# Row sums in fp32: own tiles for the pairs of the last row, and a one-element copy that takes over a wait

## Chip, cores, metric

One NeuronCore of one Trainium2 chip. The metric is device time in microseconds (us) of one execution. The runs were taken on several chips; a ratio always compares runs of the same rounds on one chip.

## The reference

```python
batch, seq, dim = 32, 512, 1024          # x: float32, normally distributed

def reference(x):
    return np.sum(x, axis=-1).astype(np.float32)
```

There are 16,384 rows of 1024 numbers, 67.1 MB to read and 64 KB to write.

## The kernel before

Each of the 128 partitions takes 128 rows, in seven tiles of 16 rows and a last tile of 16 rows that is loaded in shrinking pieces. VectorE and ScalarE sum the rows of each piece as it lands. The very last row of every partition (row 15 of the last tile) comes in two pieces that meet at column `CUT`. VectorE sums each by pairs: it adds the left half of a piece to the right half and accumulates the sums. The first sum leaves its result in `part`; the second starts from `part` and writes the final value.

```python
CUT = 576

    def pairs_dve(xt, a, b, first, acc):
        h = (a + b) // 2
        nc.vector.tensor_tensor_reduce(
            out=xt[:, a:h], in0=xt[:, a:h], in1=xt[:, h:b], scale=1.0, scalar=first,
            op0=ADD, op1=ADD, accum_out=acc,
        )
    # ... cut: the seven full tiles, and pieces of 8, 4, 2 and 1 rows of the last tile ...
    last = 15 * D
    for i, k in ((0, CUT), (CUT, D)):
        nc.sync.dma_start(
            out=xt[:, last + i : last + k],
            in_=x_b[:, c * D + last + i : c * D + last + k],
        )
    # ... cut: sums of the other rows of the last tile ...
    pairs_dve(xt, last, last + CUT, 0.0, part)
    pairs_dve(xt, last + CUT, last + D, part, res[:, c + 15 : c + 16])
    nc.sync.dma_start(out=out_b, in_=res)
```

A semaphore is a counter that a load or an engine raises when its work is done, and on which an instruction can wait. The compiled program gives each of the two sums two semaphore waits: one for its load and one for VectorE's own earlier work. In the first sum the second wait comes from writing the pairs back into `xt`; in the second it covers both that and `part`.

## Time and profile before

| | before |
|---|---|
| time, median of the three runs first given | 162.29 us (162.26 to 162.44) |
| span of the profiled run | 160.5 us |
| VectorE busy | 76% |
| HBM read | 67.11 MB |
| last load lands | 157.633 us |
| final store issued | 158.292 us |

These lines of the page of the kernel before show the busy share of each engine, the busy tenths of the DMA engines in 40 slices of the span, and the bytes moved.

```profile
DVE 122.7 (76%) x14; ACT 16.0 (10%) x29; POOL 0.2 (0%) x4
...
DMA  9979996996996996996996996996997998999991
...
HBM read 67.11 MB, written 0.07 MB: 418 GB/s over the span
```

The DMA engines are busy, or close to it, until the 39th slice ends (156.5 us). VectorE is idle for a quarter of the span. The kernel is bound by its loads.

The next lines are the end of the chain of work that ended last: start in us, duration in us, what. DVE is VectorE and ACT is ScalarE; a "q" marks an instruction of an engine's sequencer, which issues its instructions, and SPq issues the loads and the final store.

```profile
118.20 38.90 DMA xt<-in_x_dram
157.10 0.03 issue
157.13 0.02 DVEq L57
157.15 0.09 issue
157.24 0.46 DVE xt L57
157.70 0.02 DVE part L57
157.72 0.05 issue
157.77 0.45 DVE xt L57
158.22 0.01 DVEq L114
```

The first piece of the last row lands at 157.10. Then 0.14 us pass before the first sum starts at 157.24, with a short instruction of VectorE's sequencer ("DVEq") among them. That instruction is one of the two waits; both sums have one:

```profile
L57 DVEq EVENT_SEMAPHORE  x2: 21/21/21, 157.1 to 157.7; - x2
```

In the trace it holds the wait for the load, and the sum itself holds the wait for VectorE's own work.

The timeline of the same stretch has start, duration, engine, line, operation and sizes, and in brackets the idle time before.

```profile
157.24 0.46 DVE L57 CUSTOM_DVE_ANT_0 xt<-xt 128x288 f32<-128x288 f32 x1 [0.93 <-DMA xt<-in_x_dram]
...
157.62 0.08 DVE L57 DVE_READ_ACCUMULATOR2_ANT part<- 128x1 f32 x1
157.77 0.45 DVE L57 CUSTOM_DVE_ANT_0 xt<-xt,part 128x224 f32<-128x224 f32 x1
158.14 0.08 DVE L57 DVE_READ_ACCUMULATOR2_ANT res<- 128x1 f32 x1
158.29 0.35 SPq L108 DMA_DIRECT2D out_dram<-res  x1
```

Each paired sum is two instructions: the sum, and a read of its accumulator.

I use three measures throughout. They are taken to the nanosecond from the trace's instruction records and semaphore updates. L1 and L2 are the times at which the two pieces of the last row have landed (the last of the sixteen updates of that load's semaphore). The **tail** is the time from L2 to the issue of the final store: 158.292 - 157.633 = 0.659 us before.

### The profile page before, as it was taken

To read this page: it belongs to the slowest core of one execution; us is meant where nothing else is said; L and a number is where in the kernel's file an instruction comes from. 1 tells how busy PE (TensorE), PEld (TensorE's weight loads), DVE (VectorE), ACT (ScalarE), POOL (GpSimd) and SP (SyncE) were. 2 spreads that over 40 slices of the span, in tenths; PEclk is the share of its full clock that TensorE was granted. 3 is DMA by queue.
4 is the path that set the end of the run, shared out by engine and by line. 5 is a ranking of instruction groups with operands and counts; after the bars stand their busy time and mean duration, and the time that the engine had idled before them with its cause. 6 is when DMAs were issued, how large, how long until landed. Compare 5 with 4: busy or idle time off the path is not lost.

```text
span 160.5 us, 118 instructions
## 1 busy us (share of the span) xinstructions
DVE 122.7 (76%) x14; ACT 16.0 (10%) x29; POOL 0.2 (0%) x4
## 2 busy tenths in 40 slices
DVE  0000059997799959999499994999949998699992
ACT  0000000000000000000000000000000000692892
POOL 0000000000000000000000000000000000000000
DMA  9979996996996996996996996996997998999991
GB/s 376 490 306 429 490 523 261 523 523 261 523 523 261 523 523 261 523 523 261 523 523 261 523 506 278 523 506 278 523 474 310 523 425 359 392 425 425 419 401 46
DMA packets 2304, 67.18 MB, mean 418 GB/s; under 512 B 512, under 2 KB 640, under 8 KB 1024
## 3 DMA queue, kind: packets, MB, share of 16 engines
q1 hardware_dynamic: 2160, 67.12, 97.3%
q10 hardware_dynamic: 144, 0.06, 0.1%
HBM read 67.11 MB, written 0.07 MB: 418 GB/s over the span
## 4 chain that ended last, share of the span: by engine, by line
DMA 74%; DVE 22%; SPq 1%; issue 0%; DVEq 0%
DMA xt<-in_x_dram 74%; DVE res L41 21%; SPq L93 1%; DVE xt L57 1%; DVEq L57 0%; DVE part L57 0%; DVEq L114 0%
## 5 line engine op out<-in xcount | busy, mean ns | idle before, releaser
L41 DVE TENSOR_REDUCE res<-xt 128x16 f32<-128x16384 f32 (+4 forms) x10 | 121.8, 12203 | 34.5 <-DMA xt<-in_x_dram 34.5
L49 ACT ACT_TABLE_LOAD x1 | 1.3, 1283 | 137.9 <-DMA xt<-in_x_dram 137.9
L49 ACT ACTIVATE xt<-xt 128x1024 f32<-128x1024 f32 x14 | 14.6, 1042 | 3.7 <-DVE res L41 3.7
L49 ACT ACTIVATION_READ_ACCUMULATOR xt<-xt 128x1 f32 x14 | 2.6, 186 | 0.0
L57 DVE CUSTOM_DVE_ANT_0 xt<-xt 128x288 f32<-128x288 f32 x1 | 0.5, 459 | 0.9 <-DMA xt<-in_x_dram 0.9
L57 DVE CUSTOM_DVE_ANT_0 xt<-xt,part 128x224 f32<-128x224 f32 x1 | 0.5, 452 | 0.1
L151 POOL MEMSET const-uint8-127<- 128x1 uint8 x1 | 0.1, 102 | 0.0
L151 POOL MEMSET const-bfloat16-1.0<- 128x1 bf16 x1 | 0.1, 101 | 0.0
L151 POOL MEMSET const-float32-0.0<- 128x1 f32 x1 | 0.1, 98 | 0.2 <-issue 0.2
L151 POOL MEMSET const-float32-1.0<- 128x1 f32 x1 | 0.1, 98 | 0.0
L57 DVE DVE_READ_ACCUMULATOR2_ANT res<- 128x1 f32 x1 | 0.1, 84 | 0.0
L57 DVE DVE_READ_ACCUMULATOR2_ANT part<- 128x1 f32 x1 | 0.1, 83 | 0.0
## 6 DMA issues: line engine op xcount, KB each, us to landing
xt<-in_x_dram SPq DMA_DIRECT2D x1, 7680.0 KB, 21.3
xt<-in_x_dram SPq DMA_DIRECT2D x1, 4096.0 KB, 31.1
xt<-in_x_dram SPq DMA_DIRECT2D x1, 2048.0 KB, 35.7
xt<-in_x_dram SPq DMA_DIRECT2D x2, 512.0 KB, 21.1
xt<-in_x_dram SPq DMA_DIRECT2D x1, 1024.0 KB, 37.8
xt<-in_x_dram SPq DMA_DIRECT2D x1, 288.0 KB, 38.9
xt<-in_x_dram SPq DMA_DIRECT2D x1, 224.0 KB, 38.9
xt<-in_x_dram SPq DMA_DIRECT2D x6, 40.8
```

Source lines behind the costliest of these rows:

```text
L41: nc.vector.tensor_reduce(out=res[:, c : c + n], in_=xt[:, j * D : (j + n) * D].rearrange("p (j d) -> p j d", d=D), axis=X, op=ADD,)
L49: nc.scalar.activation(out=v, in_=v, func=COPY, accum_out=acc)
L57: nc.vector.tensor_tensor_reduce(out=xt[:, a:h], in0=xt[:, a:h], in1=xt[:, h:b], scale=1.0, scalar=first, op0=ADD, op1=ADD, accum_out=acc,)
L93: nc.sync.dma_start(out=xt[:, i * D : k * D], in_=x_b[:, (c + i) * D : (c + k) * D])
L151: nc = _bacc.Bacc("TRN2", target_bir_lowering=False, num_devices=1)
```

## The change

Its intent is to start the two paired sums sooner after their loads. Pairs go to tiles of their own, so that the first sum needs no wait for VectorE's own earlier instructions. A one-element copy that reads `part` waits for the carried sum in place of the second sum, which then waits for its load alone. The two pieces now meet at column 544.

```diff
-CUT = 576
+CUT = 544
@@
+    seen = rpool.tile([P, 1], F32, name="seen")
+    pairs = [rpool.tile([P, D // 2], F32, name=f"pairs{i}") for i in range(2)]
@@
-    def pairs_dve(xt, a, b, first, acc):
+    def pairs_dve(xt, a, b, first, acc, pairs):
         h = (a + b) // 2
         nc.vector.tensor_tensor_reduce(
-            out=xt[:, a:h], in0=xt[:, a:h], in1=xt[:, h:b], scale=1.0, scalar=first,
+            out=pairs[:, 0 : h - a], in0=xt[:, a:h], in1=xt[:, h:b], scale=1.0, scalar=first,
@@
-    pairs_dve(xt, last, last + CUT, 0.0, part)
-    pairs_dve(xt, last + CUT, last + D, part, res[:, c + 15 : c + 16])
+    pairs_dve(xt, last, last + CUT, 0.0, part, pairs[0])
+    nc.vector.tensor_copy(out=seen, in_=part)
+    pairs_dve(xt, last + CUT, last + D, part, res[:, c + 15 : c + 16], pairs[1])
```

More of the change, by code (lines that the diff above doesn't have):

```diff
@@ L118 @@
     sp = mybir.EngineType.SP
+    fn = tc.nc.m.functions[0]
     entry, body = None, None
-    for blk in tc.nc.m.functions[0].blocks:
+    for blk in fn.blocks:
         ops = [i for i in blk.instructions if i.engine == sp]
```

## The prediction

> **What bounds the kernel now.** The load stream. The page's totals show HBM reads of 67.1 MB in a 160.5 us span, the DMA engines 9 tenths busy or close to it in most slices until about 157 us, VectorE busy only 76%. The chain that ended last runs through loads until the first piece of the last row lands at 157.10 us. After that comes only a tail of 3.4 us: two paired sums, the 8 KB store (issued 158.29, landed 159.71), the closing barriers. The change touches nothing before 157 us but the size of the last two loads, so it can win or lose only tenths of a microsecond out of 162.29.
>
> **The tail, from the timeline and the trace's semaphore updates.** First piece (288 KB) lands 157.100; the first sum starts 157.238, 0.138 later, because it has two waits and the first is spent in a separate 0.02 us semaphore instruction of VectorE's sequencer. Reductions of the same kernel that wait on one load only start 0.023 to 0.024 after it lands (41.072 to 41.095, 137.817 to 137.841). The accumulator read starts 0.384 after the sum and signals the carried sum at 157.717. The second piece lands 157.633; the second sum starts 157.767, 0.134 after the landing and 0.05 after the carried sum: both arms bind within about 0.03 us. Its accumulator read starts 0.376 later (224 elements cost 0.233 at 0.96 GHz, so the fixed part is 0.143 against 0.084 in the first sum; it reads a carried scalar).
>
> **What the change does.** (a) Pairs go to their own tiles, so the first sum no longer waits on VectorE's own semaphore: one wait, no extra semaphore instruction, estimated 0.11 us earlier. (b) The cut moves from 576 to 544: the first piece lands about 0.04 us earlier (1.19 ns a column, from 0.533 us for 448) and its sum is 0.017 shorter. (c) The copy takes the wait on the carried sum: estimate, start 157.58, carried sum at 157.55. The Trainium skill, "VectorE: DVE Perf Modes", the section on SBUF-source ops' fixed latency, puts such an op at 58 cycles plus elements (0.06 us) and says the measured fixed term is nearer 150 cycles; this trace's reduction of 1024 elements has 0.142 fixed, and successive reductions overlap by 0.084, so I take 0.06 start to start. (d) The second sum then waits on its load only: start about 157.66 instead of 157.77, minus 0.11. (e) It has 16 elements more: plus 0.017. (f) The second load now starts at byte 2176 of a row, no multiple of 256 (2304 was). By the skill's "DMA: Bandwidth & Descriptors", "How a descriptor splits into AXI transactions", its first transaction fetches 128 unused bytes: an estimate of 4 beats in 64, up to 0.03 us; no run here shows it yet.
>
> All of (d) to (f) is on the critical path; (a) to (c) only bring the compute arm level with the landing. Net gain 0.06 to 0.09 us.
>
> **Predicted: 162.22 us**, 8 times in 10 between 162.02 and 162.42 (the three runs before already span 0.18). Faster by over 2%: 0.005; within 2%: 0.99; slower: 0.005.
>
> **What would show it.** VectorE's two sequencer semaphore instructions gone; first sum starting about 0.025 after its landing; a copy of about 0.06 to 0.15 us; second sum starting about 0.025 after its landing; its landing unchanged near 157.63, or up to 0.03 late; final store issued near 158.21.
>
> **What would make it wrong.** The copy costing 0.15 start to start, so that it and not the landing releases the second sum (gain near zero); the scalar operand's 0.06 growing without the wait; a slower last load; run-to-run scatter of 0.1 us, larger than the gain.

## The result, and the profile after

| | before | after |
|---|---|---|
| time, median of 4 runs of the same rounds | 162.37 us (162.26 to 162.58) | 162.35 us (162.18 to 162.66) |
| span of the profiled run | 160.527 us | 160.398 us |
| L1, L2 | 157.100, 157.633 | 156.999, 157.595 |
| first sum starts after L1 | 0.138 | 0.023 |
| carried sum signalled after L1 | 0.617 | 0.487 |
| second sum starts after L2 | 0.134 | 0.024 |
| its accumulator read starts after it | 0.376 | 0.394 |
| tail (L2 to store issue) | 0.659 | 0.565 |

The ratio of the times is 0.9999, 95% interval 0.9981 to 1.0018. A ratio is the mean time of one kernel's fast runs over the mean of the other's in the same rounds, so it is not quite the ratio of the medians. The times do not tell the two kernels apart. The profile does: the tail is 0.094 us shorter. The rest of the 0.129 us between the two spans is the landing of the last load, 0.038 us earlier in this run, less 0.003 us by which the store took longer. The landing's part would be within the scatter of L2 that the experiments show, but it is not only scatter. Row 14, the row before the last, landed at 156.323 before and 156.329 after, so the two pieces of the last row took 0.044 us less after the change. The section on unaligned starts comes back to this.

The page after is the same where the loads are concerned:

```profile
DVE 122.8 (77%) x15; ACT 16.1 (10%) x29; POOL 0.2 (0%) x4
...
DMA  9988996996996996996996996998999989999991
...
HBM read 67.11 MB, written 0.07 MB: 419 GB/s over the span
```

The end of the chain that ended last, after:

```profile
118.25 38.75 DMA xt<-in_x_dram
157.00 0.02 issue
157.02 0.44 DVE pairs L59
157.47 0.02 DVE part L59
157.49 0.02 issue
157.51 0.15 DVE seen L111
157.66 0.42 DVE pairs L59
158.09 0.01 DVEq L119
```

The sequencer's semaphore instruction is gone, and 0.02 us pass between the landing and the first sum. The chain view leads through the copy ("seen") because the copy is what stood last on the engine before the second sum. It is not what released it. The timeline after shows that:

```profile
157.02 0.44 DVE L59 CUSTOM_DVE_ANT_0 pairs<-xt 128x272 f32<-128x272 f32 x1 [0.69 <-DMA xt<-in_x_dram]
157.39 0.09 DVE L59 DVE_READ_ACCUMULATOR2_ANT part<- 128x1 f32 x1
...
157.51 0.15 DVE L111 COPY seen<-part 128x1 f32<-128x1 f32 x1
157.62 0.47 DVE L59 CUSTOM_DVE_ANT_0 pairs<-xt,part 128x240 f32<-128x240 f32 x1
158.01 0.08 DVE L59 DVE_READ_ACCUMULATOR2_ANT res<- 128x1 f32 x1
158.16 0.35 SPq L113 DMA_DIRECT2D out_dram<-res  x1
```

The copy starts at 157.51, and the second sum starts at 157.62 before the copy's recorded end (157.51 + 0.15). It starts 0.024 us after its load landed (157.595), the same delay as every instruction that waits on one load only. The landing released it. The later experiments show that an instruction can start 0.071 us after the start of the copy, and here it started 0.109 after.

### The profile page after: what moved, and what is told of

The parts are those of the page before. It is cut to its first block, busy times and chain, and to the rows that moved or that the text cites. A ratio compares the mean times of both kernels' runs of the same rounds, so it can differ in the third digit from the quotient of the medians.

```text
span 160.4 us, 117 instructions
## 1 busy us (share of the span) xinstructions
DVE 122.8 (77%) x15; ACT 16.1 (10%) x29; POOL 0.2 (0%) x4
## 2 busy tenths in 40 slices
DMA packets 2304, 67.18 MB, mean 419 GB/s; under 512 B 512, under 2 KB 640, under 8 KB 1024
## 4 chain that ended last, share of the span: by engine, by line
DMA 74%; DVE 22%; SPq 1%; issue 0%; DVEq 0%
DMA xt<-in_x_dram 74%; DVE res L43 21%; SPq L95 1%; DVE pairs L59 1%; DVE seen L111 0%; DVE part L59 0%; DVEq L119 0%
## 5 line engine op out<-in xcount | busy, mean ns | idle before, releaser
L59 DVE CUSTOM_DVE_ANT_0 pairs<-xt,part 128x240 f32<-128x240 f32 x1 | 0.5, 469 | 0.0
```

The source lines that it names most:

```text
L59: nc.vector.tensor_tensor_reduce(out=pairs[:, 0 : h - a], in0=xt[:, a:h], in1=xt[:, h:b], scale=1.0, scalar=first, op0=ADD, op1=ADD, accum ...
```

## The experiments

Unless said otherwise each is a single look with a profile, so its time is not compared; the tail is. In all of them the first two questions are where a sum starts after its landing, and what the tail is.

### Own tiles alone (own_tiles)

```diff
 (the changed kernel)
-CUT = 544
+CUT = 576
-    nc.vector.tensor_copy(out=seen, in_=part)
```

> Own tiles for the pairs alone, cut 576, no copy. Measured as tail = issue of the last store minus landing of the last load (before 0.659 us, changed kernel 0.565). Theory A (the two-wait instruction costs about 0.11 us per sum, and only where it is the later arm): the first sum starts 0.024 after its landing instead of 0.138, but the second sum still has two waits, so it starts 0.13 to 0.14 after its own landing and the tail stays 0.65 to 0.67. Rival B (writing in place costs time in the sums themselves, or the first sum's late start was what held the tail): tail falls by 0.05 or more.

Measured: the first sum started 0.024 us after L1 and signalled at L1 + 0.501. The second sum started 0.133 us after L2, and the tail was 0.655 us (before: 0.659). The time of this one run, 162.91 us, is not the tail's doing: its L2 was 158.238, 0.6 us later than in the profile before.

The timeline of this kernel:

```profile
157.71 0.46 DVE L59 CUSTOM_DVE_ANT_0 pairs<-xt 128x288 f32<-128x288 f32 x1 [0.75 <-DMA xt<-in_x_dram]
158.10 0.08 DVE L59 DVE_READ_ACCUMULATOR2_ANT part<- 128x1 f32 x1
...
158.37 0.45 DVE L59 CUSTOM_DVE_ANT_0 pairs<-xt,part 128x224 f32<-128x224 f32 x1 [0.19 <-DMA xt<-in_x_dram]
158.75 0.08 DVE L59 DVE_READ_ACCUMULATOR2_ANT res<- 128x1 f32 x1
```

One sequencer semaphore instruction is left, the second sum's, at 158.265. VectorE now sits idle for 0.19 us before the second sum. The carried sum was there 0.047 us before the load landed (L1 + 0.501 against L2 = L1 + 0.548), and the sum still started 0.133 after the landing. So the delay belongs to having two waits, even when the other one has been met. The first sum of the kernel before shows the same: VectorE had been idle for 0.93 us, so its earlier work was long done, and the sum still started 0.138 after its landing. Rival B falls. In all these cases the separate instruction held the load's wait. Whether the other order, with the load's wait on the sum itself, would cost the same was not tested.

### The copy alone (copy_only)

```diff
 (the kernel before)
+    seen = rpool.tile([P, 1], F32, name="seen")
     pairs_dve(xt, last, last + CUT, 0.0, part)
+    nc.vector.tensor_copy(out=seen, in_=part)
     pairs_dve(xt, last + CUT, last + D, part, res[:, c + 15 : c + 16])
```

> The copy alone, pairs still in place, cut 576. Theory A: the first sum keeps its two waits and starts 0.138 after its landing; carried sum signalled 0.62 after that landing, copy starts 0.64, next instruction may start 0.07 later, at 0.71; the second piece lands at 0.53, so the second sum starts about 0.18 after it and the tail is about 0.70, longer than before's 0.659. Rival C (the copy alone is the whole gain): second sum starts 0.024 to 0.05 after its landing, tail about 0.55 to 0.58.

Measured: tail 0.711 us, longer than before by 0.052. The compiled program shows the second sum with one wait, as intended. But the first sum kept its two waits and signalled at L1 + 0.617, and the copy started at 157.97, 0.126 after L2:

```profile
157.46 0.46 DVE L58 CUSTOM_DVE_ANT_0 xt<-xt 128x288 f32<-128x288 f32 x1 [0.91 <-DMA xt<-in_x_dram]
...
157.85 0.08 DVE L58 DVE_READ_ACCUMULATOR2_ANT part<- 128x1 f32 x1
157.97 0.15 DVE L108 COPY seen<-part 128x1 f32<-128x1 f32 x1
158.04 0.44 DVE L58 CUSTOM_DVE_ANT_0 xt<-xt,part 128x224 f32<-128x224 f32 x1
```

The second sum followed the copy's start by 0.071 us. With the carried sum late, the copy is simply one more instruction in the way. Rival C falls.

### The cut alone (cut_only)

```diff
 (the kernel before)
-CUT = 576
+CUT = 544
```

> Cut 544 alone on the kernel before. Theory A: second sum two-wait bound, starts 0.134 after its landing, 16 elements more: tail 0.67 to 0.69, no gain. Rival D (the cut is the gain): tail near 0.57.

Measured: second sum 0.134 us after L2, accumulator read 0.394 after its start, tail 0.673. The cut alone costs 0.014 us of tail, for 16 more pairs in the last sum. Rival D falls as far as the tail goes; what the cut does to L2 is told further down.

### The changed kernel with the cut put back (after_576)

```diff
 (the changed kernel)
-CUT = 544
+CUT = 576
```

> The changed kernel with the cut put back to 576. Theory A: carried sum at 0.50 after the first landing, copy at 0.53, second sum may start at 0.60; second piece lands at 0.53; so the copy and not the landing releases the second sum, about 0.04 to 0.07 after the landing; 16 elements fewer: tail 0.57 to 0.60, close to the changed kernel's 0.565 and clearly below before's 0.659. Rival D: tail back at 0.65 or more.

Measured: tail 0.592. The copy started 0.009 us after L2 and the second sum 0.071 after that, 0.080 after L2.

```profile
157.66 0.15 DVE L111 COPY seen<-part 128x1 f32<-128x1 f32 x1
157.73 0.44 DVE L59 CUSTOM_DVE_ANT_0 pairs<-xt,part 128x224 f32<-128x224 f32 x1
```

With the cut at 576 the copy sets the start; at 544 the landing does. The four kernels at cut 576 make a table of two parts:

| tail, us, cut 576 | no copy | copy |
|---|---|---|
| pairs in place | 0.659 | 0.711 |
| pairs in own tiles | 0.655 | 0.592 |

Either part alone gains at most 0.004 us or loses 0.052. Both together gain 0.067, and only with both does the cut help the tail: 0.592 to 0.565. That last step is small and rests on one profile of this kernel. The two pieces landed 0.501 to 0.548 us apart in the five profiles at cut 576, and the copy's start follows L1, so an estimate from these numbers puts this kernel's tail anywhere from 0.560 to 0.607, on either side of 0.565. The same estimate for copy_only gives 0.677 to 0.724, still no gain.

### Both kernels once more (before_again, after_again)

No edit. The kernel before was profiled again; the changed kernel was profiled and timed in five rounds.

> The kernel before, profiled once more. Theory A: the tail from last landing to store issue repeats 0.659 within 0.01 us, while the last landing itself moves by some 0.1 to 0.6 us from one run to the next (it was 157.60 to 158.24 in six runs). Rival: the tail scatters as the landing does, and then the 0.09 us between the two kernels is noise.

> The changed kernel once more, timed in five rounds. Theory A: tail 0.565 within 0.02 us; the ratio of times 0.9994 if the 0.094 us of tail were all, with an interval of at least 0.001 each way that holds 1.000, since the landing of the last load scatters by more than the gain. Rival: ratio below 0.998 or above 1.001 clear of the interval, something outside the tail.

Measured: tails 0.663 and 0.564, so each repeats within 0.004 us. In before_again the carried sum came 0.116 us after L2, and the second sum started 0.023 after it: there the carried sum and not the load set the start, and the second wait cost nothing extra. L2 was 157.784 and 157.622. Over all ten profiles of these eight kernels (the split runs left out) L2 lay between 157.595 and 158.238, a scatter of 0.6 us against a gain of 0.09. The changed kernel took 162.23 us in the median of 5 runs and the kernel before 162.43 us (9 runs): ratio 0.9991, 95% interval 0.9979 to 1.0004. This holds both 1 and the 0.9994 that 0.094 us would make.

### Without the carried sum (no_carry)

This gives a wrong result: the first piece is missing from the last row's sum.

```diff
 (the changed kernel)
-    pairs_dve(xt, last + CUT, last + D, part, res[:, c + 15 : c + 16], pairs[1])
+    pairs_dve(xt, last + CUT, last + D, 0.0, res[:, c + 15 : c + 16], pairs[1])
```

> Wrong result on purpose: the changed kernel with the second sum starting from a constant zero, not from the carried sum; the copy stays. Theory P (the fixed part of 0.143 against 0.084 us is the price of reading the carried sum as a per-partition scalar): accumulator read 0.334 after the second sum starts instead of 0.394, tail about 0.505. Rival Q (it is the price of following other short VectorE work): 0.39 and tail 0.565 as now.

Measured: accumulator read 0.335 us after the start (0.394 with the scalar), tail 0.504.

```profile
157.71 0.41 DVE L59 CUSTOM_DVE_ANT_0 pairs<-xt 128x240 f32<-128x240 f32 x1
158.04 0.08 DVE L59 DVE_READ_ACCUMULATOR2_ANT res<- 128x1 f32 x1
```

All else is equal: the sum started 0.022 after L2, and the copy was still in front of it. Reading the carried sum as a per-partition scalar costs 0.06 us. Theory P stands.

### The carried sum as one more element (carry_tail)

```diff
 (the changed kernel)
-CUT = 544
+CUT = 527
@@ the last row's second piece is loaded to a tile of its own, one column in
+    tail = rpool.tile([P, D - CUT + 1], F32, name="tail")
+    nc.sync.dma_start(out=tail[:, 1:], in_=x_b[:, at + CUT : at + D])
@@ sums
-    pairs_dve(xt, last, last + CUT, 0.0, part, pairs[0])
-    nc.vector.tensor_copy(out=seen, in_=part)
-    pairs_dve(xt, last + CUT, last + D, part, res[:, c + 15 : c + 16], pairs[1])
+    k = last + CUT - 1
+    pairs_dve(xt, last, k, xt[:, k : k + 1], tail[:, 0:1], pairs[0])
+    nc.vector.tensor_copy(out=seen, in_=tail[:, 0:1])
+    pairs_dve(tail, 0, D - CUT + 1, 0.0, res[:, c + 15 : c + 16], pairs[1])
```

(Cut: the definition of `at`, and the load of the first piece, which changes in form only.)

> A kernel meant to beat both: the carried sum is written beside the second piece's data and summed as one more element, so the second sum needs no per-partition scalar; the first sum takes its odd column as its scalar instead; cut 527. Theory P: first sum 0.06 longer, second sum may start about 0.63 after the first landing, the second piece lands 0.59 to 0.62 after it; the accumulator read comes 0.343 after the second sum starts; tail 0.51 to 0.54, time 0.9990 to 0.9994 of before, not told from 1 by the interval. Rival Q: accumulator read at 0.40, tail 0.57 or more.

Measured: the accumulator read of the first sum came 0.418 us after its start, where an estimate from the first sums without a scalar (0.084 fixed, 263 elements) is 0.36. The second sum started 0.022 after L2, with its read 0.344 later, so the tail was 0.513. The timeline shows the shorter last sum:

```profile
157.73 0.42 DVE L59 CUSTOM_DVE_ANT_0 pairs<-tail 128x249 f32<-128x249 f32 x1
158.07 0.08 DVE L59 DVE_READ_ACCUMULATOR2_ANT res<- 128x1 f32 x1
158.22 0.35 SPq L111 DMA_DIRECT2D out_dram<-res  x1
```

This has the shortest tail of all correct kernels here: 0.146 us below before and 0.052 below the changed kernel. Part of that is lost again in the landing: from row 14's landing to L2 this profile took 1.306 us and the two of the changed kernel 1.266 and 1.274. From row 14's landing to the store it is 1.819 against 1.831 and 1.838. In time it is 162.26 us against 162.43 for before in the same rounds, ratio 0.9989, interval 0.9976 to 1.0003. By time it is told from neither of the other two.

### Does an unaligned start of a load cost time? (split_576, split_544, split_512, split_608)

The changed kernel's last load starts at byte 544 x 4 = 2176 of a row, no multiple of 256. The prediction charged up to 0.03 us for it, in its step (f). Theory M below is that estimate carried over to whole rows: 128 unused bytes fetched in each row of 4096, or 3%. To make the effect large enough to time, the kernel before loads each of its seven full tiles as two column blocks, so that every row of these tiles pays for such a start.

```diff
 (the kernel before; SPLIT = 576, 544, 512 or 608)
-            parts = (0, 1, m) if done + c == 0 else (0, m)
-            for i, k in zip(parts, parts[1:]):
-                nc.sync.dma_start(
-                    out=xt[:, i * D : k * D], in_=x_b[:, (c + i) * D : (c + k) * D]
-                )
+            xs = xt.rearrange("p (r d) -> p r d", d=D)
+            bs = x_b[:, c * D : (c + m) * D].rearrange("p (r d) -> p r d", d=D)
+            for i, k in ((0, SPLIT), (SPLIT, D)):
+                nc.sync.dma_start(out=xs[:, 0:m, i:k], in_=bs[:, :, i:k])
```

> The kernel before with each full 16-row tile loaded as two column blocks, columns 0 to 576 and 576 to 1024 of all rows, so that every row of all seven tiles pays the start of a piece at byte 2304, a multiple of 256. Baseline of the three; perhaps slower than before by 0 to 5 us for its shorter runs.

> The same with the blocks meeting at column 544, byte 2176, no multiple of 256. Theory M [...]: 3% of the 135 us that the seven tiles take, about 4 us slower than the blocks at 576. Rival N (the start costs nothing where writing into the chip's memory is the limit): within 0.5 us of them.

> The same with the blocks meeting at column 512, byte 2048, a multiple of 256 and both runs alike. Both theories: within 0.5 us of the blocks at 576. If it too differs, the length of the runs and not their start decides.

> The blocks meeting at column 608, byte 2432, again no multiple of 256 and with runs of 2432 and 1664 bytes. The blocks at 544 took 171.5 us and those at 512 and 576 took 178.9, the reverse of theory M. Theory U (a second block that starts at a multiple of 256 bytes is what costs the 7.4 us): 608 goes with 544, 171 to 172 us. Rival V (544 is fast because of its two run lengths, not its start): 608 is at 175 us or more.

Measured, medians of four runs each with three rounds:

| blocks meet at column (byte) | multiple of 256 | time, us | ratio to before, 95% interval |
|---|---|---|---|
| 512 (2048) | yes | 178.90 | 1.1010 (1.0993 to 1.1026) |
| 576 (2304) | yes | 178.94 | 1.1011 (1.0994 to 1.1027) |
| 544 (2176) | no | 171.52 | 1.0557 (1.0539 to 1.0574) |
| 608 (2432) | no | 171.15 | 1.0542 (1.0525 to 1.0560) |

Theory M is refuted with the sign reversed: the cuts with unaligned starts were 7.4 us faster. Rival N, a difference of at most 0.5 us, falls too, and so does rival V of split_608. The first expectation was also missed: the blocks at 576 cost 16.5 us over the kernel before where 0 to 5 had been expected. (608 ran on another chip than the other three, where before took 162.34 instead of 162.43 us.) The rates in 40 slices, blocks at 576 first and at 544 second, show that this is the loads' rate over the whole stream and not one event:

```profile
GB/s 238 399 392 380 380 388 391 393 381 380 390 391 391 381 380 391 392 389 381 382 391 392 388 381 382 393 391 387 381 382 392 392 387 381 460 400 426 409 409 59
```

```profile
GB/s 226 411 411 407 407 410 410 408 406 407 409 409 409 407 406 409 409 408 405 408 410 410 407 406 408 409 410 405 407 407 410 410 407 405 453 494 371 407 381 31
```

The durations of single packets agree. With blocks at 544, packets of 1920 bytes took 79 ns in the median. With blocks at 576, shorter packets of 1792 bytes took the same 79 ns, although single pieces of that size in the kernel before took 74. The first blocks, which start at column 0 in every run, were slower there too: 96 ns for 2304 bytes, against 93 in the kernel before. Four cuts fit "blocks that meet at a multiple of 256 bytes are slow". They do not say why. Where the start of the second block is a multiple of 256, both block lengths are as well, so start and length are not told apart; source and destination start at the same offset in all four, so even the side is open. The queue is not ruled out either: the instruction that issues a block lasted 10.1 to 10.7 us in the median in these runs, 0.33 in the kernel before, and the chain that ended last leads through it for 72 to 73% of the span.

In the case itself there is no loss either. The last loads of the kernels at cut 576 and 544 took 74 and 79 ns a packet for 1792 and 1920 bytes, which is 24 bytes per ns in both. The mean time between the completion updates of the two pieces, over the sixteen engines, was 0.559 us for 448 columns (five profiles) and 0.586 us for 480 (four profiles): 1.25 and 1.22 ns a column, no surcharge for the unaligned start.

There is even a small gain, which the tail leaves out. From the landing of row 14 to L2, the same 1024 columns took 1.282 to 1.310 us in the five profiles at cut 576 and 1.265 to 1.274 in the four at cut 544, 0.028 less in the mean. (Taken by the mean of the sixteen updates in place of the last one, it is 1.313 to 1.322 against 1.263 to 1.266.) So the last row landed sooner with the cut at 544, in cut_only (1.265) as in the changed kernel. Why is as open as above, and carry_tail's cut at byte 2108, also no multiple of 256 but with a destination of its own, did not have it (1.306, one profile). From row 14's landing to the store, the kernel before took 1.969 and 1.945 us and the changed kernel 1.831 and 1.838: with the landing, the change is worth about 0.12 us.

## Why the prediction was right or wrong, point by point

- **What bounds the kernel.** Right. The page after is the same in loads, and 162.35 us lies in the range from 162.02 to 162.42. The time is a weak test: the kernel before took 162.37 in the same rounds, so the range would have held with no gain at all, and the 0.13 us between 162.22 and 162.35 is more than the gain forecast. The prediction is tested by the tail. A change to the last 3.4 us could move the time by tenths of a microsecond at most.
- **(a) One wait in place of two.** Right. The prediction put the gain at 0.11 us; the first sum started 0.138 after its landing before and 0.023 after. Own tiles alone then showed that this gains nothing as long as the second sum has two waits itself.
- **(b) The earlier first landing.** Right in direction, but too small. From row 14's landing to L1 the five profiles at cut 576 took 0.754 to 0.791 us and the four at cut 544 took 0.670 to 0.689, about 0.095 less in the mean, where 0.04 was charged to the cut. The shorter first sum was right: 0.016 (0.384 to 0.368) for 0.017.
- **(c) The copy.** The carried sum came 0.487 us after L1, and the prediction's 157.55 against its own landing at 157.06 makes 0.49. Start to start was put at 0.06 us; after_576 and copy_only measured 0.071. The Trainium skill, "VectorE: DVE Perf Modes", the section on SBUF-source ops' fixed latency, gives 58 cycles in a table (0.06 us) and says that the measured fixed term of a single op's duration is about 150 cycles (0.156 us). The copy's recorded duration, 0.153 to 0.155, agrees with the second. The 0.071 from start to start is near the first, but the page does not say that its table means that time.
- **(d) and (e) The second sum.** Predicted: released by its landing, about 157.66, 0.025 after the landing. Measured: 157.619, 0.024 after L2. The 16 more elements cost 0.018 (0.394 against 0.376). The 0.96 GHz that the prediction counts with comes out of the trace: reductions of 16,384 and 1,024 elements a partition took 17.220 and 1.209 us, which is 1.042 ns an element.
- **(f) The unaligned start.** Not borne out; it was put as a possible loss of up to 0.03 us. It was taken from the Trainium skill, "DMA: Bandwidth & Descriptors", "How a descriptor splits into AXI transactions", where a piece that does not start at a multiple of 256 bytes fetches unused bytes. No cost was found in the last load; the last row landed 0.028 us sooner, and with such a cut in every row the unaligned starts were the faster ones by 7.4 us. Whether the unused bytes are fetched no run here shows. In these runs they were not what set the time.
- **Net.** 0.06 to 0.09 us was predicted. The tail as it is measured here does not contain (f), which would move L2; without (f) the prediction's sum is 0.11 - 0.017 = 0.093, and the tails show 0.094 (0.099 in the repeats, 0.663 - 0.564). With the last row landing 0.028 sooner, where (f) had up to 0.03 later, the gain is about 0.12, more than was predicted; that part was not foreseen.
- **What would make it wrong.** "Run-to-run scatter of 0.1 us, larger than the gain" was too small a figure: the landing of the last load alone scattered by 0.6 us over ten profiles. That the gain is real is shown by the tail, in four profiles of the two kernels. It is not shown by the times. A gain of 0.06 to 0.07% cannot be told from none by ratios with intervals of 0.13% to 0.18% each way.

The experiments add what the prediction only stated: the parts of the change depend on each other. A sum with two waits started 0.133 to 0.138 us after its load wherever the load set its start, so both sums needed one wait each. Moving the cut then let the copy start before the second piece landed (0.027 us of tail, with one profile of after_576) and brought the landing of the last row forward.

## What to carry to other kernels

Where the stretch after the last load is what you tune, measure from the landing of that load, and from the last landing that the change cannot move; the time of the whole run carries the loads' scatter and hides 0.1 us. A sum that waited for two semaphores, with the load's wait in a separate instruction, started 0.11 us later than one that waited for a load alone, even with the other wait met 0.8 us before the load landed. So let an earlier instruction take one of the waits, provided that instruction starts early enough: the copy here by some 0.05 us before the landing (an estimate, 0.071 less 0.024). A carried sum that is read as a per-partition scalar cost 0.06 us in the last instruction; stored beside the data as one more element it cost one element there (the first sum took a scalar instead, off the critical path).

## What the Trainium skill lacked or had wrong

- "VectorE: DVE Perf Modes", section "The DRAIN you can't avoid", says that a semaphore after each of a chain of copies costs nothing extra. It does not give the price of a second wait on one instruction: here 0.133 to 0.138 us from landing to start with two waits, 0.022 to 0.024 with one.
- "DVE: scalar operands, raw-bit mode, write accounting and state across instructions", section 1, says a bf16 scale costs the same as an fp32 one, but not what a per-partition scalar costs over a constant: here 0.06 us (0.394 against 0.335 to the accumulator read).
- "VectorE: DVE Perf Modes", the section on SBUF-source ops' fixed latency, gives 58 cycles plus elements in a table, and about 150 cycles as the measured fixed term of one op's duration. It does not say how soon the next op can start: here a one-element fp32 copy lasted 0.153 to 0.155 us, and the next sum could start 0.071 us after it started.
- "DMA: Bandwidth & Descriptors", "How a descriptor splits into AXI transactions", counts extra beats for starts off a multiple of 256 bytes: here row blocks that meet at bytes 2176 and 2432 took 171.52 and 171.15 us, and those that meet at 2048 and 2304 took 178.90 and 178.94, and the last row landed 0.028 us sooner with its cut at byte 2176 than at 2304. No page has this, and its cause is open.
